# The down projection's fifth block product made as seven of halved blocks, and two products' activations stored split

## The chip, the core and the metric

The program runs on one core of one Trainium2 chip. The metric is device microseconds of one execution. The engines are named as in the profile: PE is TensorE's matmul, PEld its weight load, DVE is VectorE, ACT is ScalarE, POOL is GpSimd, SP issues most of the DMAs. Lnnn is a line of the kernel before, unless a passage says that it shows the kernel after.

## The reference, cut to what matters

SEQ and D_MODEL are 1024, D_FF is 4096, and everything is float32. The block's first sub-layer (a gated mixer of pooling and attention) gives x; the change is all in the second:

```python
h2 = _rmsnorm(x, g_mlp_pre[l])
ff = jnp.einsum('bsf,fd->bsd',
                jnp.square(jax.nn.relu(jnp.einsum('bsd,df->bsf', h2, w_up[l]))), w_down[l])
x = x + _rmsnorm(ff, g_mlp_post[l])
```

Below, x1 is x ahead of this sub-layer, f the squared relu (4096 by 1024, stored by columns of D_FF), and w the down weights.

## The kernel before

**Stages.** The mixer runs to about 470 us of the profiled execution, the up part, which makes f, to about 779, and the down part, which makes ff and the output, to the end.

**Precision.** PE gets operands that are split in two: a rounded high half, which ACT casts (L101), and the rest, which DVE subtracts (L104). A product of two such operands takes three passes: high by high, and the two mixed ones. Every split of 128x1024 thus costs a cast on ACT and a subtraction on DVE.

**Seven block products.** The down matrix product, 2 by 2 blocks, is made as seven block products with sums of blocks for operands (the Winograd form), in place of eight. The seven are numbered 1 to 7 and run in the order of the list `PRODUCTS`, which before is 1, 5, 2, 3, 6, 7, 4. Each goes over the inner dimension in eight steps (NS = 8). A step of a normal product loads one block of f and one of w, 128x1024 each, splits both, and makes 24 matmuls of 128x512 (`down_mm`, L2075) into four PSUM banks. There are 56 steps, numbered j = 0 to 55 through the products.

**One halved product.** The sixth product is again made as seven products of halved blocks (`quarters`, `quarters_mm` L2055, `quarters_close`): 42 matmuls of 128x256 in a step instead of 24 of 128x512, into seven half banks. Its step needs four splits: f1 (the block of f, 1024 elements), f2 (three sums of quarters of f, 768, made in the up part and kept in `spill`), w1 (three quarters of w, 512 and 256), and w2 (four sums of quarters of w, 1024, called T). The T sums are three DVE operations of 512, 256 and 256 (L2009 to L2011), each needing the one before. When its last step is done, `quarters_close` adds the seven results into u with one ACT copy and eight DVE operations (L2062 to L2069).

**Who adds to whom.** The second product is added onto the banks of the first, the third onto those of the fifth. ACT copies the banks out at their ends: u from the first, v from the fifth, c11 from the second, c12 from the third. After the sixth and seventh, DVE sums these (`after_sixth`, `after_seventh`).

**Sums of weight blocks.** The blocks of w stay in SBUF as B11, B12, B21, B22 (eight of each, pool rp of 24 tiles). The fifth needs B12 - B11 (L1978, in its own steps); near the end of the third `differences` makes B22 - B11 and B22 - B12 (L2005, L2007) and the T sums; `last_weights` (L2016) takes one more difference during the seventh and fourth.

**Order and buffers.** Operands of step j+2 are issued in step j (AHEAD = 2). Split operands of f lie in pool wp (six slots "wh"), those of w in pool ga (six), raw blocks from DRAM in four buffers "raw". A load into a buffer, or a split into a slot, waits until its last reader is done. A scheduler orders each engine's instructions, except for stretches under `manual_schedule`, where the named engines run in the written order: DVE from the sixth product on, and PE, ACT and DVE for the sixth's last step and close.

**Up part.** f is made tile by tile in pairs. A function `store` for each pair, run a little later, makes the sums of blocks of f that the down products need and stores them to `f_dram`: seven blocks of 512 columns for each pair, the eighth of them (the sums for f2) to `spill`. While a tile is made, DVE also sums and splits the up weights.

**x1.** In the fifth product's steps `square_x1` loads a tile of x1 into a raw buffer and ACT squares it (L2104), for the last norm.

## Time and profile before

| | |
|---|---|
| median of 3 runs | 1090.79 us (1090.67 to 1090.97) |
| the profiled execution | 1091.0 us, its span 1089.2 |
| mean granted clock of TensorE | 0.999 |
| up part, 470 to 779 us | PE busy 309.00 of 309.00, DVE 219.74, ACT 174.85 |
| down part, 779 to the end | PE busy 302.35 of 310.20, DVE 237.48, ACT 163.05 |

The chain of waits is a list of stretches of work, each released by the one above; a row has its start, its length and what it was. A row of a timeline has the start, the length, the engine, the line, the operation with output and inputs by name, its shape and how many alike followed each other; a bracket tells how long the engine had been idle before it and what ended that. A row of a table of windows has, for each window, its length and then PE, PEld, DVE, ACT and POOL's busy time in it. The costliest groups have busy time, mean ns of one instruction, and the idle time before the group's instructions with what ended it. Of DMA issues, the last number is the median time in us from issue to landing.

### The profile page before, as it was taken

What the parts mean: (1) busy time and instruction counts of PE and PEld (TensorE: products, weight loads), DVE (VectorE), ACT (ScalarE), POOL (GpSimd) and SP (SyncE); (2) the same over time, 40 slices, a digit from 0 to 9 for tenths busy, and PEclk for the clock granted to TensorE, in tenths of its full rate; (3) what the DMA queues carried; (4) which work ended last, traced back from release to release, by engine and by line L of the source; (5) the groups of instructions that cost most, each with busy time, mean ns of one, the idle gap of its engine ahead of it and who ended that gap; (6) DMA issues with size and microseconds to landing.
All of it is one profiled execution on the core that took longest, in us unless ns stands there. A gap on an engine that the chain in (4) does not pass through costs nothing.

```text
span 1089.2 us, 14332 instructions
## 1 busy us (share of the span) xinstructions
PE 1079.7 (99%) x5211; PEld 903.5 (83%) x5211; DVE 849.2 (78%) x1194; ACT 625.5 (57%) x1029; POOL 86.2 (8%) x142
## 2 busy tenths in 40 slices
PE   9999999999999999999999999999999999999997
PEld 8888888888888888888888888888888888898885
DVE  6688888989897887889876766665657867579996
ACT  7567886456654257567665554555446535476543
POOL 0354411100100012100000000000000000000000
PEclk9999999999999999999999999999999999999999
DMA  9666889679965776832566534445597873379622
GB/s 333 201 174 175 214 251 350 184 233 315 268 213 171 223 191 137 288 117 77 185 227 227 205 143 174 160 150 216 177 391 272 299 265 118 101 234 318 218 78 78
DMA packets 100921, 227.36 MB, mean 209 GB/s; under 512 B 10481, under 2 KB 28017, under 8 KB 100849
## 3 DMA queue, kind: packets, MB, share of 16 engines
q1 hardware_dynamic: 84416, 189.46, 50.8%
q0 software_dynamic: 10528, 16.78, 8.8%
q10 hardware_dynamic: 5904, 20.19, 4.8%
q8 instruction: 41, 0.67, 0.3%
q14 instruction: 32, 0.25, 0.1%
HBM read 161.38 MB, written 63.97 MB: 207 GB/s over the span
## 4 chain that ended last, share of the span: by engine, by line
PE 75%; DVE 4%; ACT 1%; issue 1%; DMA 1%; ACTq 0%; DVEq 0%
PE mm L583 18%; PE at L583 15%; PE at L2075 12%; PE mm L2075 11%; PE mm L1523 5%; PE mm L494 3%; PE at L2055 2%; PE at L1523 2%; PE at L1251 2%; PE mm L2055 2%; PE mm L1251 1%; PE mm L496 1%; PE at L1569 1%; DMA st<-in_w_g_dram 1%; DVE xf L2121 0%
## 5 line engine op out<-in xcount | busy, mean ns | idle before, releaser
L2075 PE MATMUL at<-ar,wh 128*128 128x512 f32 x552 | 126.0, 389 | 0.2 <-DVE ar L104 0.2
L2075 PEld LDWEIGHTS at<-ar,wh 128*128 128x128 f32 x552 | 103.4, 188 | 22.1 <-DVE ar L104 0.6
L2075 PE MATMUL mm<-ar,wh 128*128 128x512 f32 x528 | 120.5, 389 | 0.0
L2075 PEld LDWEIGHTS mm<-ar,wh 128*128 128x128 f32 x528 | 99.1, 188 | 20.5
L101 ACT CAST wh<-raw 128x1024 fp32r<-128x1024 f32 (+1 forms) x58 | 59.2, 1023 | 86.2 <-PE at L2075 37.0
L104 DVE TENSOR_TENSOR wh<-st,wh 128x512 fp32r<-128x512 f32 (+1 forms) x103 | 74.4, 733 | 38.9 <-ACT wh L101 34.3
L104 DVE TENSOR_TENSOR wh<-raw,wh 128x1024 fp32r<-128x1024 f32 (+1 forms) x58 | 68.4, 1186 | 40.8 <-ACT wh L101 40.6
L583 PE MATMUL mm<-T,wx 128*128 128x512 f32 x375 | 90.3, 389 | 0.0
L583 PEld LDWEIGHTS mm<-T,wx 128*128 128x128 f32 x375 | 70.4, 188 | 14.6
L583 PE MATMUL mm<-gr,wh 128*128 128x512 f32 x321 | 77.2, 391 | 0.0
L101 ACT CAST wh<-st 128x512 fp32r<-128x512 f32 (+2 forms) x102 | 65.8, 654 | 19.2 <-PE at L583 4.6
L583 PEld LDWEIGHTS mm<-gr,wh 128*128 128x128 f32 x321 | 59.9, 188 | 12.2
L583 PE MATMUL mm<-T,wh 128*128 128x512 f32 x267 | 66.0, 389 | 0.0
L104 DVE TENSOR_TENSOR ar<-B,ar 128x1024 fp32r<-128x1024 f32 (+2 forms) x51 | 50.9, 1011 | 14.7 <-ACT ar L101 14.4
L583 PE MATMUL at<-gr,wh 128*128 128x512 f32 x243 | 59.0, 389 | 0.0
L583 PE MATMUL mm<-x,wh 128*128 128x512 f32 x240 | 58.9, 394 | 0.0
L583 PEld LDWEIGHTS mm<-T,wh 128*128 128x128 f32 x267 | 50.1, 188 | 10.4
L101 ACT CAST ar<-B 128x1024 fp32r<-128x1024 f32 (+2 forms) x51 | 44.1, 882 | 19.3 <-PE mm L2055 6.4
L583 PEld LDWEIGHTS at<-gr,wh 128*128 128x128 f32 x243 | 45.6, 188 | 9.5
L583 PEld LDWEIGHTS mm<-x,wh 128*128 128x128 f32 x240 | 44.2, 188 | 9.6 <-ACT f L692 0.2
L583 PE MATMUL at<-T,wx 128*128 128x512 f32 x213 | 52.0, 389 | 0.0
L583 PEld LDWEIGHTS at<-T,wx 128*128 128x128 f32 x213 | 40.0, 188 | 8.3
(529 smaller groups left out, 2264.5 us busy)
## 6 DMA issues: line engine op xcount, KB each, us to landing
raw<-f_dram SPq DMA_DIRECT2D x52, 512.0 KB, 4.7
B<-in_w_dn_dram SPq DMA_DIRECT2D x32, 512.0 KB, 6.5
f_dram<-g SPq DMA_DIRECT2D x28, 512.0 KB, 2.8
st<-in_w_up_dram SPq DMA_DIRECT2D x24, 512.0 KB, 4.5
g<-spill_dram SPq DMA_DIRECT2D x17, 512.0 KB, 5.7
f_dram<-g ACTq DMA_DIRECT2D x17, 512.0 KB, 2.9
st<-in_w_g_dram SPq DMA_DIRECT2D x16, 512.0 KB, 4.7
g<-in_w_up_dram SPq DMA_DIRECT2D x15, 512.0 KB, 4.8
```

The source lines that it names most:

```text
L101: act.copy(hi, src)
L104: return eng.tensor_tensor(lo, src, f32(hi), ALU.subtract)
L494: pe.matmul(bs[th], whi[:, k, :], rhs(k, hl, th), start=k == 0 and hl == 0, stop=False)
L496: pe.matmul(bs[th], wlo[:, k, :], rhs(k, 0, th), start=False, stop=k == nk - 1)
L583: pe.matmul(b, w[wh][:, kt, :], x_, start=not after and kt == 0 and j == 0, stop=kt == 3 and j == 2, skip_group_check=after)
L1251: pe.matmul(b, w[wh][:, kt, :], xo[xh][:, kt, :], start=not after and kt == 0 and j == 0, stop=kt == 1 and j == 2, skip_group_check=after)
L1523: pe.matmul(bs[t], Am[a][k][ah][:, t * P:(t + 1) * P], Wm[w][k][wh], start=not after and k == 0 and j == 0, stop=k == 3 and j == 2, skip_g ...
L1569: pe.transpose(b[:, i, :], hs[4 * th + i][:, k * P:(k + 1) * P], ident)
L2055: pe.matmul(part[q][:, t, :], o[fs][fh][:, fk, t * P:(t + 1) * P], o[ws][wh][:, wk, :], start=q not in ONTO and (s_, t, j) == (0, 0, 0), s ...
L2075: pe.matmul(bs[t], fo[fh][:, k2, t * P:(t + 1) * P], wo_[wh][:, k2, :], start=not after and s2 == 0 and k2 == 0 and j == 0, stop=(s2, k2) ...
```

## The change

**Order.** The products run as 1, 2, 5, 3, 6, 7, 4, so that the second follows the first, and the fifth, now halved like the sixth, comes behind these two. Steps 0 to 15 are the first and second, 16 to 23 the fifth, 24 to 31 the third, 32 to 39 the sixth, 40 to 47 the seventh, 48 to 55 the fourth. The fifth's close makes v in seven DVE operations; the third has banks of its own and is added to v by DVE at its end (c12).

**Split activations.** `store` splits two more blocks, those of the seventh and the third, and stores both halves: nine blocks for a pair. For these products the halves are loaded straight into slots "wh", and no split of f is made in the down part. It also makes the quarter sums for the fifth's f2.

**Placement.** All of the down part's DVE work but the last step is now in the written order. Loads of weight blocks (`loads`), sums of weight blocks (`sums`) and the rest (`ends`, among it the x1 squares, now in steps 24 to 31) are each given step numbers.

```diff
     def store():
...
-                dve.tensor_tensor(s2[:, 256:], s2[:, :256], s2[:, 256:], ALU.subtract)
-                s2_even.append(s2)
+                for b in (t[:, 0, :], s2):
+                    dve.tensor_tensor(b[:, 256:], b[:, :256], b[:, 256:], ALU.subtract)
+                evens.append(t)
             else:
...
+                for i, a, b in ((5, t0[:, 0, :], t[:, 0, :]), (6, t0[:, 1, :], s2)):
+                    e = g32([3, 256])
+                    dve.tensor_tensor(e[:, 1, :], b[:, 256:], a[:, 256:], ALU.subtract)
+                    dve.tensor_tensor(e[:, 0, :], e[:, 1, :], a[:, :256], ALU.add)
+                    dve.tensor_tensor(e[:, 2, :], b[:, :256], e[:, 1, :], ALU.subtract)
+                    q.dma_start(e_dram(i, m // 4), e)
+            q.dma_start(fd[:, 5:7, :], t)
+            q.dma_start(fd[:, 0, :], f[:, :512])
+            for c, src in ((1, f[:, 512:]), (7, s4)):
+                parts = gr([2, 512])
+                split(parts[:, 0, :], parts[:, 1, :], src)
+                q.dma_start(fd[:, c:c + 2, :], f32(parts))
...
+    WITH_PARTS = (7, 3)
...
     def operands(i, s_):
-        if i == 1 and s_ in early_raw:
+        if i in WITH_PARTS:
+            fo = wslot([2, 512]), wslot([2, 512])
+            for c, t in enumerate(fo):
+                behind[:] = [nc.sync.dma_start(f32(t), f_block(A_OF[i] + c, s_))]
+            ft = None
...
-        split(*fo, ft)
-        behind[:] = [split(*wo_, wt)]
+        if ft is not None:
+            split(*fo, ft)
+        split(*wo_, wt)
...
+    def first_sum(s_):
+        dve.tensor_tensor(res["B11", s_], res["B12", s_], res["B11", s_], ALU.subtract)
+
+    def next_sum(n, s_):
+        dve.tensor_tensor(res[n, s_], res["B22", s_], res[n, s_], ALU.subtract)
...
-            elif i == 5:
-                act.copy(v[t], bs[t])
...
-    PRODUCTS = (1, 5, 2, 3, 6, 7, 4)
+    PRODUCTS = (1, 2, 5, 3, 6, 7, 4)
+    HALVED = (5, 6)
...
+    LOADS = (("B11", 4, 3), ("B12", 5, 8), ("B22", 15, 8), ("B21", 41, 8))
...
+    def sums(j):
...
+        if at(8):
+            first_sum(j - 8)
+        if at(9):
+            quarter_sums(j - 9)
+        if at(18):
+            next_sum("B12", j - 18)
+        if at(22):
+            next_sum("B11", j - 22)
+        if at(24):
+            quarter_sums(j - 24)
+        if at(42):
+            last_sum(j - 42)
...
+    def ends(j):
...
+        if 24 <= j < 24 + NS:
+            square_x1(j - 24)
...
+    def down_step(j, i, s_):
...
+        if i in HALVED and last:
+            with tc.manual_schedule(engines=CORE):
+                quarters_mm(i, s_)
+                quarters_close(i)
+            ahead(j)
+            sums(j)
...
+        else:
+            sums(j)
+            ahead(j)
+        loads(j)
...
-    fd = nc.dram_tensor("f_dram", (NF // 2, P, 7, 512), F32, kind="Internal").ap()
+    fd = nc.dram_tensor("f_dram", (NF // 2, P, 9, 512), F32, kind="Internal").ap()
```

Three places in the order of instructions. The first is DVE behind the fifth's close in the kernel after, steps 23 and 24, where L104 is the subtraction of a split, L2009 a sum of weight blocks (`next_sum`), and L2017 to L2019 the T sums:

```order
L104 TENSOR_TENSOR ar_8395<-B_1247_7896,ar_8394 128x1024
L2009 TENSOR_TENSOR B_1189_7609<-B_1298_8170,B_1189_7609 128x1024
L2009 TENSOR_TENSOR B_1150_7400<-B_1247_7896,B_1150_7400 128x1024
L2009 TENSOR_TENSOR B_1197_7652<-B_1309_8237,B_1197_7652 128x1024
L2009 TENSOR_TENSOR B_1158_7440<-B_1265_7969,B_1158_7440 128x1024
L2017 TENSOR_TENSOR T_8402<-B_1143_7362 128x512
L2018 TENSOR_TENSOR T_8402<-B_1143_7362,T_8402 128x256
L2019 TENSOR_TENSOR T_8402<-B_1143_7362,T_8402 128x256
L104 TENSOR_TENSOR ar_8411<-B_1265_7969,ar_8410 128x1024
```

Before, the same sums (L2005, L2007) stand in the second and third products, where the scheduler put them among the splits of f and w (here those of the second):

```order
L2007 TENSOR_TENSOR B_1154_7473<-B_1255_8087,B_1154_7473 128x1024
L2005 TENSOR_TENSOR B_1105_7199<-B_1261_8123,B_1105_7199 128x1024
L104 TENSOR_TENSOR wh_7750<-raw_7745,wh_7749 128x1024
L104 TENSOR_TENSOR ar_7752<-raw_7747,ar_7751 128x1024
L2007 TENSOR_TENSOR B_1161_7513<-B_1261_8123,B_1161_7513 128x1024
```

So the sums moved to the end of the halved fifth and the start of the third, and four of them and a T now stand between the weight splits of steps 25 and 26.

The second place is ACT at the end of the fifth in the kernel after. L2116 is a square of x1, L2069 the copy that opens the close:

```order
L101 CAST wh_8219<-raw_8217 128x768
L2116 ACTIVATE raw_8442,nsq<-raw_8442 128x1024
L101 CAST wh_8229<-raw_8215 128x1024
L101 CAST ar_8227<-B_1145_7390 128x512
L101 CAST ar_8227<-B_1145_7390 128x256
L101 CAST ar_8287<-B_1235_7840 128x1024
L2116 ACTIVATE raw_8485,nsq<-raw_8485 128x1024
L2116 ACTIVATE raw_8527,nsq<-raw_8527 128x1024
L2069 COPY st_8379<-mm_7900 128x512
```

The first square moved from the normal fifth to a place between the cast of f2 and those of f1 and w1 of step 23, and two more stand ahead of the copy.

The third place is DVE behind the first `store` of the up part, with the splits of the up weights (wx, wh). Before:

```order
L1631 TENSOR_TENSOR g_5075<-f_first,g_5074 128x512
L104 TENSOR_TENSOR wx_5118<-ws_5112,wx_5118 128x512
L1635 TENSOR_TENSOR g_5074<-g_5074 128x256
L613 TENSOR_TENSOR g_5097<-g_5097,at_5084 128x512
L104 TENSOR_TENSOR wx_5122<-st_5055,wx_5122 128x512
```

And after:

```order
L1631 TENSOR_TENSOR g_5075<-f_first,g_5074 128x512
L1636 TENSOR_TENSOR g_5074<-g_5074 128x256 x2
L104 TENSOR_TENSOR gr_5084<-g_4608,gr_5084 128x512
L104 TENSOR_TENSOR wx_5126<-ws_5120,wx_5126 128x512
L104 TENSOR_TENSOR wx_5130<-st_5055,wx_5130 128x512
L104 TENSOR_TENSOR gr_5088<-g_5075,gr_5088 128x512
```

The two splits of `store` (gr) stand among those of the next weights, one of them ahead of wx.

## The prediction

> **What bounds the kernel now.** I read first the page's busy times, then the chain of waits, then the timelines of TensorE and VectorE where the products of the last stage meet.

> ```profile
> span 1089.2 us, 14332 instructions
> PE 1079.7 (99%) x5211; PEld 903.5 (83%) x5211; DVE 849.2 (78%) x1194; ACT 625.5 (57%) x1029; POOL 86.2 (8%) x142
> ```

> TensorE is busy for 99% of the span, so time can only go where matmuls go, and any wait that the change lets TensorE see is added whole. VectorE has 22% free on average; that says nothing about one stage. The chain of waits (start, length, what) shows what a product of the last stage costs:

> ```profile
> 822.82 43.52 PE mm L2075 x192
> 866.34 43.52 PE at L2075 x192
> 909.86 43.52 PE mm L2075 x192
> 953.38 2.87 PE at L2055 x24
> ...
> 993.85 4.30 PE at L2075 x19
> 998.15 1.14 DVE wh L104
> 999.28 1.15 DVE ar L104
> 1000.47 37.47 PE at L2075 x164
> ```

> A normal product is 192 matmuls in 43.52 us, 226.7 ns each and 5.44 us a step. The sixth, the halved one, begins at 953.38 and its successor's first matmul is in the timeline of TensorE:

> ```profile
> 993.69 6.58 PE L2075 MATMUL at<-ar,wh 128*128 128x512 f32 x28
> 1000.47 2.79 PE L2075 MATMUL at<-ar,wh 128*128 128x512 f32 x11 [0.21 <-DVE ar L104]
> ...
> 1037.78 4.47 PE L2075 MATMUL mm<-ar,wh 128*128 128x512 f32 x19
> ```

> The sixth takes 993.69 - 953.38 = 40.31 us: 336 matmuls of 128x256 at 120 ns, 5.04 us a step. The seventh, from 993.69 to 1037.78, takes 44.09 us where 43.52 would do; 0.57 us is lost in its second step, which waited for VectorE. What VectorE did there:

> ```profile
> 993.15 0.68 DVE L2062 TENSOR_TENSOR st<-st,at 128x512 f32<-128x512 f32 x1
> ...
> 997.46 0.68 DVE L2069 TENSOR_TENSOR u<-u,st 128x512 f32<-128x512 f32 x1
> 998.06 1.22 DVE L104 TENSOR_TENSOR wh<-raw,wh 128x1024 fp32r<-128x1024 f32 x1
> 999.20 1.22 DVE L104 TENSOR_TENSOR ar<-B,ar 128x1024 fp32r<-128x1024 f32 x1
> 1000.34 1.22 DVE L104 TENSOR_TENSOR wh<-raw,wh 128x1024 fp32r<-128x1024 f32 x1
> ```

> The eight operations of the close take 4.91 us, and the splits of the next step's two operands stand behind them. Operations in a row follow each other in 1.14 us though each lasts 1.22: 0.08 us of each lies beside its neighbour. So a 128x1024 operation costs 1.14 in a row, and by the same overlap a 128x512 one 0.61, a 128x256 one 0.34.

> **How full VectorE is in a halved product**, by its timeline in one step of the sixth:

> ```profile
> 968.51 1.03 DVE L104 TENSOR_TENSOR ar<-B,ar 128x512 fp32r<-128x512 f32 x2
> 969.45 2.10 DVE L104 TENSOR_TENSOR wh<-raw,wh 128x1024 fp32r<-128x1024 f32 x2
> 971.47 1.22 DVE L104 TENSOR_TENSOR ar<-T,ar 128x1024 fp32r<-128x1024 f32 x1
> 973.54 1.03 DVE L104 TENSOR_TENSOR ar<-B,ar 128x512 fp32r<-128x512 f32 x2 [0.86 <-ACT ar L101]
> ```

> A step's splits take w1 0.95, f1 1.14, f2 0.87 and w2 1.14: 4.10 of 5.04 us, and 0.86 is idle, in which it waits for TensorE to free a buffer. VectorE is about half a step ahead, no more, since the operand buffers hold no more.

> **The change, part by part.** The sum starts from the profiled execution's own 1091.0 us (1.8 outside its span); the median of the runs is 1090.79, so the two agree within 0.02%.

> (1) The fifth product has 336 matmuls of 128x256 in place of 192 of 128x512: 43.52 - 40.32 = **-3.20 us**. A matmul of half the columns costs 120 ns and not 113.3, so 2 x 120 - 226.7 = 13.3 ns of each is fixed by these rows. [...]

> (2) The seventh's activations come split from DRAM, so of the three splits behind the sixth's close only that of the weights is left. The wait of **-0.57** goes. What is late next there is the load itself: the two halves of a step go straight into operand buffers that are free only when the step two before has run, so the first block of the seventh has 5.04 us.

> ```profile
> raw<-f_dram SPq DMA_DIRECT2D x52, 512.0 KB, 4.7
> raw<-x_dram SPq DMA_DIRECT2D x8, 512.0 KB, 5.1
> ```

> Two such loads, issued behind each other on SP, land 4.7 us after issue or a little later: 0 to 0.8 us of wait, no less than nothing as no buffer is free sooner. I take **+0.4**, between the ends. VectorE's and ACT's saved splits in the third and seventh are off the path, beyond the stretch in (4).

> (3) The fifth now follows the second, whose end ACT copies out (four copies and four squares) ahead of the fifth's casts. The timeline of ACT shows that pattern after the second in before:

> ```profile
> 909.11 1.06 ACT L2248 COPY c<-at 128x512 f32<-128x512 f32 x2
> ...
> 911.68 0.21 ACT L2081 ACTIVATION_READ_ACCUMULATOR junk<-c 128x1 f32 x1
> 911.77 1.05 ACT L101 CAST wh<-raw 128x1024 fp32r<-128x1024 f32 x1
> ```

> There a cast stood until 911.77, some 2 us into the next product, with nobody waiting. A halved step needs its f1 2.4 us after its start. So the first step can wait 0 (if casts slip in between) to 0.95 us (two more squares ahead); I take **+0.35**.

> (4) The stretch from the fifth into the third is the term that decides. The sums of weight blocks (one 128x1024 operation each, 1.14) are now placed by step number: one in each of steps 18 to 21, two in each of 22 to 25, and from step 24 on also the sums for the sixth's T:

> ```profile
> 907.72 0.69 DVE L2009 TENSOR_TENSOR T<-B 128x512 f32<-128x512 f32 x1
> 908.44 0.42 DVE L2010 TENSOR_TENSOR T<-B,T 128x256 f32<-128x256 f32 x1
> 908.90 0.42 DVE L2011 TENSOR_TENSOR T<-B,T 128x256 f32<-128x256 f32 x1
> 909.25 0.69 DVE L2084 TENSOR_TENSOR c<-c,bc 128x512 f32<-128x512 f32 x1
> ```

> Each of these waits for the one before, so the three take 1.53. VectorE's order is fixed as written, so I add it from the start of step 19 to the split that step 26 needs: w1 and f1 of 19, 2.1; four times a sum and a step's splits, 4 x (1.14 + 4.10) = 21.0; two sums, 2.3; the weights of step 24, 1.1; the fifth's close, seven operations, 4.3; the weights of 25, 1.1; four sums, 4.6; T, 1.5; the weights of 26, 1.2. That is 39.2 us. TensorE uses up in the same stretch five halved steps, two normal ones and the four matmuls that stand ahead of the first one needing that split: 5 x 5.04 + 2 x 5.44 + 0.9 = 37.0. So TensorE waits **+2.2 us**, spread over steps 21 to 26. The low end is 0, if some of those sums find idle time that I have not seen; the high end counts all 43 operations at full length instead of overlapped, 43 x 0.08 = 3.4 more, 5.6 in all. I take 2.2, because the rows at 998.06 to 1000.34 show the overlap in just such a run of operations.

> (5) The squares of x1 move from the fifth's steps, where they were in a normal product, to steps 24 to 31, and are recorded so that the first stands on ACT ahead of the casts of step 23's f1 and w1, and two more ahead of the copy that opens the close. Their loads go through the same four raw buffers.

> ```profile
> L2104 ACT ACTIVATE raw<-raw 128x1024 f32<-128x1024 f32 x8 | 8.5, 1060 | 4.8 <-DMA raw<-x_dram 4.8
> ```

> ACT already sat 4.8 us for these loads in before, with a normal product around it as cover. Behind the waiting square are now the casts for step 23, for which TensorE waits 2.4 us into it; on SP the first blocks of the third wait behind the x1 loads. The load is issued once f2 of step 22 is split, 5.1 us before it lands. What of this goes beyond the 2.2 of (4) is bounded by 0 (ACT waits while VectorE is late anyway) and 1.7 (step 23 alone waits 2.25, 0.55 of which is in (4)); **+0.5**, nearer to the lower end because both waits fall in the same steps.

> (6) The up part splits two blocks more in every pair of tiles and makes one or three more 128x256 sums: 2 x 0.61 + 2 x 0.34 = 1.9 us of VectorE a pair, 2.2 where nothing overlaps, and two casts on ACT. The two pairs at 500 to 537 have almost nothing free (the columns behind the bounds are PE, weight load, VectorE, ACT):

> ```profile
> 500.00:518.00 18.00, 18.00 (x85) 15.00 (x84) 18.00 (x25) 12.09 (x18) 0.00 (x0) 1.00 0.30 91
> 518.00:537.00 19.00, 19.00 (x85) 15.74 (x84) 17.80 (x31) 13.48 (x22) 0.00 (x0) 1.00 0.46 167
> 537.00:556.00 19.00, 19.00 (x85) 15.73 (x85) 10.96 (x20) 10.75 (x17) 0.00 (x0) 1.00 0.67 233
> ```

> 1.2 us are free in those 37 and 3.8 to 4.4 are added; 8.0 are free in the 19 behind. If the late work is the stores', it drains there and costs nothing; if weight splits wait behind it, up to 3.2. I take **+0.5**.

> Sum: 1091.0 - 3.20 - 0.57 + 0.4 + 0.35 + 2.2 + 0.5 + 0.5 = 1091.2 us. Most of what TensorE no longer does, it waits.

> **The rivals.**
> - VectorE keeps up. The waits of (4), (5) and (6) are hidden: 1091.2 - 2.2 - 0.5 - 0.5 = 1088.0. For it: the 849.2 us of VectorE leave room on both sides of the stretch. Against it: its order is fixed, and nothing lets it start a step's splits earlier than the buffers come free.
> - The x1 squares hold ACT, ending slower: the first square waits for its load while step 23's casts stand behind it, and the copy of the close behind two more. It decides from the point where the load lands later than 2.4 us into step 23 less two casts. Then (5) costs 2.5 and not 0.5: 1093.2. For it: the 4.8 us row above. Against it: three of the raw loads ahead could be early.
> - The up part's backlog reaches TensorE: 2.6 instead of 0.5, 1093.3. For it: the windows at 500 to 537. Against it: those windows hold work that can be put off, and TensorE had no gap there.
> - Every small operation pays its full length in the stretch: (4) costs 5.6, 1094.6. [...] The rows of the close at 993.15 to 998.06 speak against it, since they overlap.

> That the fifth isn't halved at all is excluded by the order of TensorE's instructions, which has 336 of 128x256 for it.

> **How the numbers follow.** A measurement of this kernel can tell about 0.2%, 2.2 us, from no change. The forecast, 1091.2, has 0.38 and lies within it (1088.6 to 1093.0). VectorE keeping up, 1088.0, has 0.29 and is faster by more. The x1 squares have 0.17, the up part 0.11, full-length operations 0.05; these three are slower by more, 0.33 together. The range reaches from a little under the first rival, 1087.4, to a little over the fourth's 1094.6, 1095.4: it leaves out at its low end the case that nothing waits at all, 1087.2, and at its high end two rivals at once.

> **What would show it.** In the profile of the changed kernel the fifth should take 40.3 us plus its own waits. (4) is right if TensorE's idle time in the second half of the fifth and the first three steps of the third is near 2 us and is ended by VectorE's splits of weights; if ACT's cast or an x1 load ends it, (5) was the greater. (2) is right if the seventh's first step waits for a load for less than a microsecond and its second step not at all. (6) shows as idle TensorE between 500 and 560, released by VectorE. The forecast is wrong if VectorE has idle time within the stretch, or if TensorE's gaps stand somewhere else altogether, such as in the second product, where sums for the fifth are now made.

## The result, and the profile after

The changed kernel takes **1109.44 us** (median of 4 runs, 1107.02 to 1112.63) against 1090.79 before: a ratio of 1.0173, 95% interval 1.0147 to 1.0199. It is 1.7% slower, and outside the predicted range.

The page of the changed kernel, its first lines and the row of TensorE's clock:

```profile
span 1107.8 us, 14938 instructions
PE 1086.9 (98%) x5355; PEld 911.4 (82%) x5355; DVE 893.0 (81%) x1301; ACT 637.9 (58%) x1062; POOL 84.4 (8%) x142
...
PEclk9999999999999999999989999999999999999998
```

VectorE has 44 us more to do and ACT 12. TensorE's busy time went up by 7.2 us although its matmuls need 3.2 us less: some of them ran slower. There is an 8 in the row of the clock, in the 21st slice, near 560 us, where before there was a 9. Where the 18.6 us of span are, from the starts of stages in TensorE's timelines:

```profile
789.65 2.88 PE L583 MATMUL at<-ar,wh 128*128 128x512 f32 x12
792.38 4.42 PE L2087 MATMUL at<-gr,wh 128*128 128x512 f32 x18
...
883.28 3.04 PE L2061 MATMUL mm<-ar,wh 128*128 128x256 f32 x24
...
1011.64 0.70 PE L2087 MATMUL mm<-ar,wh 128*128 128x512 f32 x2
```

L583 is the up part, L2087 a normal down product, L2061 a halved one.

| stretch | before | after | difference |
|---|---|---|---|
| to the end of the up part (779.14; after: 792.38, less six down matmuls that stand among those of the up part, 1.36 us) | 779.1 | 791.0 | +11.9 |
| first and second normal product | 87.0 | 92.3 | +5.2 |
| the next three products (before: two normal and the sixth, 866.2 to 993.7; after: the fifth, third and sixth) | 127.5 | 128.4 | +0.9 |
| the last two and the end | 95.5 | 96.2 | +0.7 |

Before, the second place in the row "first and second" was the fifth's; both are normal products. The place that the prediction was about, the third row, came out 1 us above its forecast there. Nearly all of the loss stands ahead of it. TensorE's gaps there, from its timeline:

```profile
565.08 0.73 PE L583 MATMUL mm<-T,wx 128*128 128x512 f32 x2 [3.10 <-ACT wx L101]
568.32 4.21 PE L583 MATMUL mm<-T,wh 128*128 128x512 f32 x9 [1.82 <-ACT g L612]
...
597.51 0.73 PE L583 MATMUL mm<-T,wx 128*128 128x512 f32 x2 [0.44 <-ACT wx L101]
599.80 3.91 PE L583 MATMUL mm<-T,wh 128*128 128x512 f32 x9 [1.03 <-ACT g L612]
...
809.99 0.73 PE L2087 MATMUL at<-ar,wh 128*128 128x512 f32 x2 [2.32 <-ACT ar L101]
811.25 4.14 PE L2087 MATMUL at<-ar,wh 128*128 128x512 f32 x10 [0.53 <-DVE ar L104]
```

Four gaps in the up part make 6.4 us, two in the first product 2.85. Behind the gaps matmuls are slow: nine in 4.21 us, where nine take 2.0. The table of windows of TensorE alone (length, busy time, granted clock, DMA share, GB/s) shows why:

```profile
564.00:566.00 2.00, 0.92 (x4) 1.00 0.35 131
566.00:568.00 2.00, 0.50 (x2) 0.50 0.00 0
568.00:570.00 2.00, 1.68 (x4) 0.50 0.71 276
570.00:572.00 2.00, 2.00 (x6) 0.50 1.01 391
572.00:574.00 2.00, 2.00 (x9) 0.80 0.97 315
```

The gap begins at 561.98 (565.08 - 3.10); from 566 on the clock stands at half, and it is back at full near 572.8 (0.80 is the mean of that row): some 7 us. So the gaps cost 6.4 us in the up part and what follows them 5.5 more; in the first product 2.85 and 2.4. What follows is half clock (10.2 us of it in the up part, 3.4 in the first product, half of which is lost) and a slower start behind each gap (two matmuls in 0.73 us at 565.08 and 597.51, where two at 561.36, ahead of the first gap, took 0.61).

**The first gap.** It ends with ACT's cast of a sum of up weights (L532, L535), and that sum needs a weight load. SP's queue in the changed kernel:

```profile
555.10 0.92 SPq L1651 DMA_DIRECT2D f_dram<-gr  x2
556.13 1.26 SPq L523 DMA_DIRECT2D g<-in_w_up_dram  x1
```

and in the kernel before:

```profile
551.40 0.48 SPq L523 DMA_DIRECT2D g<-in_w_up_dram  x1
551.99 0.58 SPq L523 DMA_DIRECT2D st<-in_w_up_dram  x1
553.99 0.33 SPq L523 DMA_DIRECT2D g<-in_w_up_dram  x1
```

The load (L523) into a buffer g is issued 4.7 us later, behind the two stores of split halves (L1651), and the next one, at 553.99 before, only at 569.56. The pool of these buffers has 17, and each pair of tiles now takes two more of them, until the stores have landed; but no weight load between 480 and 780 us is seen to wait for the landing of such a store.

The late load alone doesn't explain the gap. VectorE's timeline at the sum, in the changed kernel:

```profile
561.56 0.69 DVE L625 TENSOR_TENSOR g<-g,at 128x512 f32<-128x512 f32 x1 [5.15 <-PE at L583]
562.62 0.69 DVE L532 TENSOR_TENSOR ws<-g 128x512 f32<-128x512 f32 x1 [0.37 <-DMA g<-in_w_up_dram]
```

The sum waited 0.37 us for its load, and ACT, busy without a break from 562.28 on, came to the cast 0.38 us after the sum was made. Before, the same chain, from L625 at 556.30 to the cast at 559.03, is as long (2.7 against 2.85 us), but TensorE has 12 matmuls (at<-T,wx, from 556.10) to make meanwhile. In the changed kernel these 12 ran at 550.53 already, ahead of those on wh, whose operand ACT's copy L612 made at 555.11: it stands behind the two casts of stored halves, which waited 2.41 us for VectorE's sums. Before it was made at 549.00. The gaps of 1.82 and 1.03 us end with this copy too, again behind these casts.

**Why the gap in the first product.** What SP waited for between 780 and 812 us in the changed kernel, the longest row (total, times, longest), and the first weight load of the down part in its timeline:

```profile
SPq L1962 <- DVE g L1644: 12.3, 1, 12.3
```

```profile
802.86 0.38 SPq L1962 DMA_DIRECT2D B<-in_w_dn_dram  x1
```

The load's tile lies over the buffer of the last store's quarter sums (L1644); when they were made, it waited 2.7 us more, until they had landed in `spill`. It went out at 802.86, 11.9 us after the up part's end; before, at 784.77, 5.6 us after, for there another buffer lay under it.

### The profile page after: what moved, and what is told of

Same layout as the page of the kernel before. It is cut to its first block, busy times and chain, and to the rows that moved or that the text cites. A ratio compares the mean times of both kernels' runs of the same rounds, so it can differ in the third digit from the quotient of the medians.

```text
span 1107.8 us, 14938 instructions
## 1 busy us (share of the span) xinstructions
PE 1086.9 (98%) x5355; PEld 911.4 (82%) x5355; DVE 893.0 (81%) x1301; ACT 637.9 (58%) x1062; POOL 84.4 (8%) x142
## 4 chain that ended last, share of the span: by engine, by line
PE 88%; DVE 5%; DMA 4%; ACT 2%; issue 1%; SPq 0%; DVEq 0%; ACTq 0%
PE mm L583 25%; PE at L583 17%; PE at L2087 12%; PE mm L2087 6%; PE mm L1523 5%; PE at L2061 3%; PE mm L494 3%; PE mm L2061 3%; PE sc L182 2%; PE at L1523 2%; PE at L1251 2%; PE mm L191 2%; PE mm L182 2%; PE mm L1251 1%; PE mm L496 1%; DMA wh<-f_dram 1%
## 5 line engine op out<-in xcount | busy, mean ns | idle before, releaser
L2087 PE MATMUL at<-ar,wh 128*128 128x512 f32 x588 | 144.2, 393 | 4.2 <-ACT ar L101 2.3
L2087 PEld LDWEIGHTS at<-ar,wh 128*128 128x128 f32 x588 | 111.2, 190 | 29.0 <-ACT ar L101 4.3
L104 DVE TENSOR_TENSOR wh<-st,wh 128x512 fp32r<-128x512 f32 (+1 forms) x103 | 74.9, 736 | 38.8 <-ACT wh L101 34.7
L583 PE MATMUL mm<-T,wx 128*128 128x512 f32 x375 | 92.0, 390 | 3.5 <-ACT wx L101 3.5
L583 PEld LDWEIGHTS mm<-T,wx 128*128 128x128 f32 x375 | 70.7, 189 | 19.1 <-ACT wx L101 4.4
L101 ACT CAST wh<-raw 128x1024 fp32r<-128x1024 f32 (+1 forms) x50 | 48.9, 981 | 55.5 <-PE at L2087 40.8
L583 PE MATMUL mm<-gr,wh 128*128 128x512 f32 x321 | 77.2, 391 | 0.0
L101 ACT CAST wh<-st 128x512 fp32r<-128x512 f32 (+2 forms) x102 | 65.9, 653 | 19.3 <-DVE st L539 6.0
L2087 PE MATMUL mm<-ar,wh 128*128 128x512 f32 x300 | 76.9, 390 | 0.1
L583 PE MATMUL mm<-T,wh 128*128 128x512 f32 x267 | 70.4, 407 | 2.9 <-ACT g L612 2.9
L104 DVE TENSOR_TENSOR wh<-raw,wh 128x1024 fp32r<-128x1024 f32 (+1 forms) x50 | 56.4, 1136 | 17.5 <-ACT wh L101 17.3
L583 PEld LDWEIGHTS mm<-gr,wh 128*128 128x128 f32 x321 | 59.9, 188 | 12.2
L101 ACT CAST ar<-B 128x1024 fp32r<-128x1024 f32 (+2 forms) x59 | 42.8, 757 | 43.2 <-DMA B<-in_w_dn_dram 10.7
L2087 PEld LDWEIGHTS mm<-ar,wh 128*128 128x128 f32 x300 | 56.2, 188 | 12.3 <-DMA wh<-f_dram 0.5
L104 DVE TENSOR_TENSOR ar<-B,ar 128x1024 fp32r<-128x1024 f32 (+2 forms) x59 | 49.3, 859 | 20.5 <-ACT ar L101 20.4
L583 PEld LDWEIGHTS mm<-T,wh 128*128 128x128 f32 x267 | 51.9, 196 | 15.7 <-ACT g L612 4.8
L583 PE MATMUL at<-gr,wh 128*128 128x512 f32 x243 | 59.0, 389 | 0.0
L583 PE MATMUL mm<-x,wh 128*128 128x512 f32 x240 | 58.9, 394 | 0.0
L583 PEld LDWEIGHTS at<-gr,wh 128*128 128x128 f32 x243 | 45.6, 188 | 9.5
L583 PE MATMUL at<-T,wx 128*128 128x512 f32 x213 | 53.1, 390 | 0.0
L583 PEld LDWEIGHTS mm<-x,wh 128*128 128x128 f32 x240 | 44.2, 188 | 9.6 <-ACT f L692 0.2
L2061 PE MATMUL mm<-ar,wh 128*128 128x256 f32 x336 | 47.5, 285 | 0.7 <-DVE ar L104 0.4
## 6 DMA issues: line engine op xcount, KB each, us to landing
raw<-f_dram SPq DMA_DIRECT2D x36, 512.0 KB, 4.3
B<-in_w_dn_dram SPq DMA_DIRECT2D x32, 512.0 KB, 6.4
wh<-f_dram SPq DMA_DIRECT2D x32, 512.0 KB, 5.2
f_dram<-gr SPq DMA_DIRECT2D x30, 512.0 KB, 4.2
st<-in_w_up_dram SPq DMA_DIRECT2D x24, 512.0 KB, 4.3
g<-spill_dram SPq DMA_DIRECT2D x17, 512.0 KB, 5.7
st<-in_w_g_dram SPq DMA_DIRECT2D x16, 512.0 KB, 5.3
f_dram<-g ACTq DMA_DIRECT2D x16, 512.0 KB, 2.7
```

Source lines behind the costliest of these rows:

```text
L101: act.copy(hi, src)
L104: return eng.tensor_tensor(lo, src, f32(hi), ALU.subtract)
L583: pe.matmul(b, w[wh][:, kt, :], x_, start=not after and kt == 0 and j == 0, stop=kt == 3 and j == 2, skip_group_check=after)
L2061: pe.matmul(part[q][:, t, :], o[fs][fh][:, fk, t * P:(t + 1) * P], o[ws][wh][:, wk, :], start=q not in onto and (s_, t, j) == (0, 0, 0), s ...
L2087: pe.matmul(bs[t], fo[fh][:, k2, t * P:(t + 1) * P], wo_[wh][:, k2, :], start=not after and s2 == 0 and k2 == 0 and j == 0, stop=(s2, k2) ...
```

## The experiments

Each time stands against the kernel before, run on the same chip (1090.4 to 1090.9 in each set). Where a kernel has the down part of the change, "the stretch" is from the fifth's first matmul to the sixth's end: 128.4 us in the change, 124.2 by its matmuls (2 x 40.32 + 43.52). Kernels with the same down part differed there by up to 2 us (128.4 to 130.3), so less is not read.

**1. The stored splits, away.** Blocks stored whole, and split in the down part again:

```diff
-            q.dma_start(fd[:, 0, :], f[:, :512])
-            for c, src in ((1, f[:, 512:]), (7, s4)):
-                parts = gr([2, 512])
-                split(parts[:, 0, :], parts[:, 1, :], src)
-                q.dma_start(fd[:, c:c + 2, :], f32(parts))
+            q.dma_start(fd[:, 0:2, :], f.rearrange("p (a b) -> p a b", b=512))
+            q.dma_start(fd[:, 7, :], s4)
...
-    WITH_PARTS = (7, 3)
+    WITH_PARTS = ()
```

> The change, but the blocks of f for the third and seventh are stored whole as before and split in the down part again; all else as changed (fifth halved, order, sums, x1). Theory A (the loss is made in the up part by the stored splits, directly and by the half clock behind the gaps): TensorE has no gap between 540 and 640 us, the up part ends at 779 to 781 us as in the kernel before, and the time falls by 10 or more, to about 1095 (3.2 gained by the halving, about 7 lost in the stretch from the fifth to the third, where three more splits of 1.14 come in). Theory B (the loss comes from halving the fifth and the written order of the down part): the time stays above 1104.

Measured: 1095.94 (ratio 1.0045, 1.0028 to 1.0062). No gap in the up part, which ends where it ended before. The fifth starts at 866.26, as the third product in order does before. All 17 us ahead of the fifth are the stored splits'. The waits of TensorE from 480 us on are in the down part:

```profile
PE at L2084 <- DVE ar L104: 4.1, 3, 2.6
PE mm L2058 <- DVE ar L104: 0.4, 1, 0.4
```

So Theory A holds. It leaves 5 us: without split blocks VectorE is late in the third, and the stretch is 132.6.

**2. The stores on GpSimd's queue.**

```diff
-                q.dma_start(fd[:, c:c + 2, :], f32(parts))
+                nc.gpsimd.dma_start(fd[:, c:c + 2, :], f32(parts))
```

> The change, with the two stores of split halves of each pair issued by GpSimd's queue and not by SP's or ACT's. If SP's order is what delays the up weights (their load stands behind two stores that wait for the splits): the gaps at 562 to 568 and 597 to 600 us go or halve, the up part ends at 780 to 785 us, time about 1098 to 1102. If it is the buffers (a weight load waits for a buffer that a store frees on landing, and stores on GpSimd's queue land no earlier): gaps as before or longer, time 1107 or more.

Measured: 1103.21 (1.0111, 1.0095 to 1.0126), 6 us less than the change. The up part's gaps shrank to 3.7 us in all (1.9, 1.0, 0.8) and its last matmuls start 5.5 us sooner (784.16 for 789.65). Here the sum L532 waited 6.67 us for its weight load, and the gap of 1.9 followed. With the stores off SP's queue about half of the up part's loss goes (5 of 11.9 us), a third of the whole; the first product's gap of 2.3 us stays.

**3. Other memory under the first load.**

```diff
+    pool.memset(held("pad")[:, 0, :], 0.0)
+    pool.memset(raw_tile()[:, 0, :], 0.0)
     with tc.manual_schedule(engines={mybir.EngineType.DVE}):
```

> The change, with one unused weight tile and one unused raw tile allocated (and cleared by GpSimd) ahead of the down part, so that the first weight load of the first product gets memory that is long free and not that of the last store's sums. If SP stood still until 802.86 us for that memory: the first such load is issued by 800 at the latest, the gap of 2.3 + 0.5 us at 808 to 811 goes with the half clock behind it, and the time falls by about 5, to 1104. If the load was late for another reason (the queue's other waits, the DMA engines): unchanged within 1.

Measured: 1104.48 (1.0134, 1.0114 to 1.0153), 5.0 less. In its trace the first load is issued at 796.04, and of the gap 0.19 us is left:

```profile
813.08 2.14 PE L2087 MATMUL at<-ar,wh 128*128 128x512 f32 x8 [0.19 <-DVE ar L104]
```

The fifth starts at 878.31, 5.0 us sooner, 0.45 of it from the up part. So the memory under the first tiles was the cause of 4.5 of the 5.2 us in the second row of the table. The execution that was profiled is the slowest of the four, 1108.81: behind the fifth's start it lost again what it had gained, 130.3 us in the stretch and 1.54 at the seventh's start.

**4 and 5. What a gap costs.** First, idle operations put into VectorE's order in the kernel before:

```diff
             with given(i):
+                for _ in range({1: 10, 5: 14}.get(s_, 0)):
+                    dve.tensor_tensor(c11[3], c11[3], c11[3], ALU.max)
```

> The kernel before, with 10 and 14 idle operations of VectorE (128x512, 0.61 us each in a row) put ahead of the splits in the second and sixth steps of the seventh product; results unchanged. If a gap costs only itself, the time rises by the idle time of TensorE that the trace shows, and the granted clock stays 1.00. If a gap of some 2 us or more is followed by a stretch at half clock, as at 566 to 573 us in the changed kernel, the windows behind it show a clock near 0.5 for 3 to 6 us and the time rises by the idle time plus half of that, about 2 us more for each gap.

Measured: 1091.53, and no gap: the scheduler moved these operations, which hang on nothing, ahead into idle time. It decides nothing. Then on the loaded block itself:

```diff
+        for _ in range({(7, 3): 6, (4, 1): 10}.get((i, s_), 0)):
+            dve.tensor_tensor(ft, ft, ft, ALU.max)
         split(*fo, ft)
```

> The kernel before, with 6 idle operations of VectorE (1.14 us each) on the block of f of the seventh's fourth step and 10 on that of the fourth's second step, results unchanged. If a gap costs only itself, the granted clock stays at 1.00 behind the gaps and the time rises by TensorE's idle time. If a gap of over 2 us is followed by half clock, the windows behind show 0.5 for 3 to 6 us, and the time rises by the idle time and about 2 us more for each such gap.

Measured: 1109.28, +18.9. TensorE's timeline at its gaps, and the table of windows behind the first one:

```profile
1014.61 2.07 PE L2077 MATMUL at<-ar,wh 128*128 128x512 f32 x4 [4.08 <-ACT wh L101]
1017.01 28.42 PE L2077 MATMUL at<-ar,wh 128*128 128x512 f32 x116 [0.32 <-DVE ar L104]
1053.36 1.20 PE L2077 MATMUL mm<-ar,wh 128*128 128x512 f32 x4 [2.49 <-ACT wh L101]
1055.75 29.50 PE L2077 MATMUL mm<-ar,wh 128*128 128x512 f32 x116 [1.20 <-DVE ar L104]
```

```profile
1014.00:1016.00 2.00, 1.39 (x3) 0.54 0.00 0
1016.00:1018.00 2.00, 1.68 (x4) 0.50 0.49 94
1018.00:1020.00 2.00, 2.00 (x6) 0.50 1.03 371
1020.00:1022.00 2.00, 2.00 (x8) 0.76 0.95 316
```

The four gaps are 8.1 us of the 18.9. Behind each of the two pairs TensorE stood at half clock for 6.8 us, which costs 3.4 each time, more than the 2 us that were expected; some 3 us more stand behind the last matmul, where VectorE's own work came late. So in a kernel that has none of the change, a wait alone brings the half clock. It begins some 3.5 us after the first gap's start (1014.61 - 4.08 = 1010.53, and 0.54 from 1014 on). The second pair brought it too, though its gaps are of 2.49 and 1.20 us, with 1.2 us of matmuls between them: no single wait as long as the first's 4.08 was needed.

**6. One buffer for both high halves**, the low halves written over their blocks:

```diff
...
+            high = gr([2, 512])
+            for c, src in ((0, f[:, 512:]), (1, s4)):
+                split(high[:, c, :], src, src)
+            q.dma_start(fd[:, 0:2, :], f.rearrange("p (a b) -> p a b", b=512))
+            q.dma_start(fd[:, 8, :], s4)
+            q.dma_start(fd[:, 6:8, :], f32(high))
```

> The change, with each pair's stored splits written otherwise: the low halves over the blocks they come from, both high halves in one buffer, so that a pair takes one buffer of the pool more than before the change and not two, and four stores of halves and blocks instead of four plus one; the same splits on ACT and VectorE. If buffers and the number of stores ahead of the weight loads make the up part's gaps: the gaps shrink to under 2 us in all, the up part ends at 779 to 783 us, time 1098 to 1101. If the additional work of VectorE and ACT makes them: the gaps stay near 6 us and the time at 1107 or more.

Measured: 1109.83 (1.0174, 1.0157 to 1.0191), no gain in all. The up part's gaps fell to 4.2 us (3.2 and 1.0), and its last matmuls start 5.2 us sooner; but the first load of the down part still went out at 802.76, since its tile lay over a buffer of stored halves until these had landed, and that gap grew to 5.8:

```profile
SPq L1963 <- DMA f_dram<-gr: 11.1, 1, 11.1
```

One loss was exchanged for another.

**7 to 9. The stretch from the fifth to the sixth.** Sums of weights later; x1 loads behind those of f; both:

```diff
-        if at(18):
-            next_sum("B12", j - 18)
+        if at(22):
+            next_sum("B12", j - 22)
```

```diff
-        nc.sync.dma_start(t, x1_dram[n])
+        with tc.issue_after(behind[0].ins):
+            nc.sync.dma_start(t, x1_dram[n])
```

> The change, with the sums B22 - B12 placed in steps 22 to 29 and not 18 to 25: four sums fewer (4.6 us of VectorE) ahead of the weights' split of step 26. The stretch from the first matmul of the fifth to the end of the sixth took 128.3 us in the changed kernel where its matmuls need 124.2. If VectorE's sums set that loss: 124.5 to 126, and VectorE has idle time in the fifth. If the x1 loads and squares set it: 128 or more, with the wait for the blocks of f at the start of the third as before.

> The change, with each x1 load issued behind the loads of f for the third, so that no square stands on ACT ahead of step 23's casts. If the x1 loads and squares set the loss of 4.1 us in the stretch from the fifth to the sixth's end: the wait of 1.34 us for the first blocks of the third goes, ACT's idle 0.71 us of VectorE too, and the stretch takes 125 to 126.5 us. If VectorE's sums set it: 127.5 or more, with waits that VectorE's splits end.

> The change, with the later sums and the later x1 loads together. Theory: each of the two hides the other, since either alone left the stretch from the fifth to the sixth's end at 127.5 to 129.4 us (128.3 in the changed kernel). Then both together take it to 125 to 126, near the 124.2 of its matmuls. If something else sets it (the loads of split blocks, TensorE's own order): 127.5 or more again.

Measured, times 1110.62, 1110.52 and 1105.17 (one run each, beside a change that varies from 1107.0 to 1112.6); the stretch 128.4, 127.5 and 127.0. Fewer sums alone bring nothing. The later x1 loads bring 1 us, and both 1.4, under what was expected (125 to 126). With x1 later, the wait of 1.34 us for the first blocks of the third went and a wait for VectorE's split of 1.1 us came in the third:

```profile
938.95 0.74 PE L2087 MATMUL at<-ar,wh 128*128 128x512 f32 x2 [1.10 <-DVE ar L104]
```

So each hid a part of the other; some 3 us stay above the matmuls' time with both.

**10 and 11. Can the kernel with whole blocks win?** T sums from step 26, or the sums B22 - B12 on GpSimd:

```diff
-        if at(24):
-            quarter_sums(j - 24)
+        if at(26):
+            quarter_sums(j - 26)
```

```diff
-        dve.tensor_tensor(res[n, s_], res["B22", s_], res[n, s_], ALU.subtract)
+        eng = pool if n == "B12" else dve
+        eng.tensor_tensor(res[n, s_], res["B22", s_], res[n, s_], ALU.subtract)
```

> The kernel with whole blocks stored (unsplit), the later x1 loads, and the sums for the sixth's T placed in steps 26 to 33 and not 24 to 31. The loss of unsplit against its matmuls stood in the third, where VectorE's splits ended waits of 4.1 us and half clock followed. If VectorE's order there was the cause: the waits at 909 to 925 us fall to under 1 us and the time to 1088 to 1091. If VectorE simply has too much work in that stretch, wherever it stands: 1093 or more.

> The kernel with whole blocks stored, the later x1 loads, and the eight sums B22 - B12 made by GpSimd and not VectorE (9 us of VectorE less in the fifth and third). If VectorE's amount of work sets the loss and GpSimd does a sum in 5 us or less: the waits in the third fall to 1 to 2 us and the time to 1088 to 1091. If GpSimd is slower, or slows VectorE beside it: 1093 or more.

Measured: 1095.37 (1.0042, 1.0027 to 1.0057) and 1102.67 (1.0107, 1.0090 to 1.0124). With later T sums the waits in the third fell to 2.5 us and the sixth got 1.6 us of new ones: VectorE has too much to do there, wherever it stands. GpSimd made a sum in 2.6 to 2.7 us, fast enough, and yet this was 7 us slower than whole blocks without it (experiment 1, which differs in the x1 loads too). VectorE's and GpSimd's timelines beside each other:

```profile
889.61 2.08 DVE L104 TENSOR_TENSOR wh<-raw,wh 128x1024 fp32r<-128x1024 f32 x2
891.61 3.39 DVE L104 TENSOR_TENSOR ar<-T,ar 128x1024 fp32r<-128x1024 f32 x1
```

```profile
891.32 2.61 POOL L2007 TENSOR_TENSOR B<-B,B 128x1024 f32<-128x1024 f32 x1 [1.92 <-DVE wh L104]
```

VectorE's subtraction, 1.22 us at 884.83 and at 898.03, took 3.39 when it was started while GpSimd's sum ran, and ended behind it. Both operations read two tensors of SBUF.

**12. All remedies at once**: 3, 6, 9 and the later T sums, in one kernel.

> The change with all of its losses taken on at once: one buffer for the high halves, unused tiles ahead of the first weight loads, later sums, later x1 loads, T sums from step 26. If the losses found are all there are and they add up: the up part ends at about 787 (gaps of 4 us and half clock stay), no gap in the first product, 125 to 126 us from the fifth to the sixth's end; time 1094 to 1098. If taking one away shows another behind it: 1102 or more.

Measured: 1101.70 (1.0104, 1.0089 to 1.0119), 7.7 less than the change and above the expected 1094 to 1098. The fifth starts at 874.43, 8.9 us sooner than in the change; the stretch is 127.4; but from the sixth's end on it takes 98.8 us where the change takes 96.2, with a new wait of 1.8 us for VectorE in the fourth. The losses add up only in part.

**13 to 15. What a stored split does to the up part.** To the kernel with whole blocks, one thing each was added: the splits' work, into a free half of a buffer; as many and as large stores; or the two buffers, with splits and stores of 16 columns.

```diff
...
+            for src in (f[:, 512:], s4):
+                act.copy(spare.bitcast(F32R), src)
+                dve.tensor_tensor(spare.bitcast(F32R), src, spare, ALU.subtract)
...
```

```diff
             q.dma_start(fd[:, 0, :], f[:, :512])
...
+            q.dma_start(fd[:, 1:3, :], f.rearrange("p (a b) -> p a b", b=512))
+            q.dma_start(fd[:, 7, :], s4)
+            q.dma_start(fd[:, 8, :], s4)
...
```

```diff
+            for src in (f[:, 512:], s4):
+                parts = gr([2, 512])
+                split(parts[:, 0, :16], parts[:, 1, :16], src[:, :16])
+                q.dma_start(fd[:, 8, :32].rearrange("p (a b) -> p a b", b=16), f32(parts[:, :, :16]))
...
```

> The kernel with whole blocks stored (unsplit, 1095.9 us, no gap in the up part), with the two splits of each pair made on ACT and VectorE all the same, into a free half of a buffer, and not stored or used. If the up part lost its 11.9 us by the work of ACT and VectorE: gaps near 560 and 600 us, time 1102 or more. If by buffers and queue alone: no gap over 0.5 us in the up part, time 1095 to 1098 (the later end of the last store may delay the first product by 1 or 2).

> The same kernel with as many and as large stores for each pair as in the change (a second store of a block's two halves and of the sums, 0.5 MB more a pair... of what lies there), no splits and no more buffers. If the stores' number and bytes on SP's queue make the loss: gaps near 560 and 600 us, time 1102 or more. If not: no gap over 0.5 us, 1095 to 1098.

> The same kernel with two more buffers taken for each pair, as in the change, each with a split and a store of 2 x 16 columns only: the buffers are held until that store lands, and the stores stand in SP's queue behind the splits, but neither work nor bytes are added to speak of. If the weight loads wait for buffers and behind those stores: gaps of 3 us or more near 560 us, time 1102 or more, even though nothing else is added. If not: 1095 to 1098, and the loss needs all three together.

Measured: 1098.08, 1097.62 and 1104.61 (1.0065, 1.0062 and 1.0130; the last one's interval 1.0113 to 1.0147). The fifth starts at 867.5, 867.6 and 873.7, against 866.3 with whole blocks and 883.3 in the change. Work alone costs 1.2 us, of which 0.1 in the up part; stores alone cost 1.3, all in the up part; buffers with almost nothing in them cost 7.4, 5.4 of it there. TensorE's waits from 480 to 860 us in the last kernel:

```profile
PE mm L583 <- ACT g L612: 1.6, 1, 1.6
PE at L583 <- ACT wx L101: 1.0, 1, 1.0
...
PE mm L583 <- ACT f L603: 0.7, 1, 0.7
...
PE mm L583 <- ACT wx L101: 0.5, 1, 0.5
```

The gaps stand at 563 to 595 us, as in the change, but half clock followed none of them (clock 1.00 in every 10 us from 540 to 1090). One at a time the three make 10 of the 17 us; the other 7 come when they are together, and the half clock of the change (5.5 and 2.4 with the slow starts) is of that size.

The 7.4 can't all be put down to buffers. Both small stores of a pair go to the same columns of `f_dram`, so that the second stands on SP until the first has landed, which the change hasn't. What SP waited for from 480 to 780 us in this kernel:

```profile
SPq L1650 <- DMA f_dram<-gr: 14.5, 14, 2.3
```

And the longest gap, 1.58 us, ends with ACT's copy L612, which stands behind the two casts of 16 columns as it does behind the full ones in the change; with work alone the scheduler put this copy ahead of the second cast, where it ran at 550.90, as early as with whole blocks (551.01). Each of these kernels was ordered anew, and none holds the order still. So how the up part's loss divides among buffers, the stores' place on SP and the casts' place on ACT stays open.

None of these kernels is faster than the kernel before; the best, with whole blocks and later T sums, is 0.4% slower.

## Why the prediction was wrong

It said 1091.2 us, range 1087.4 to 1095.4. By its own steps:

(1) The halved fifth: right. Its matmuls take the 120 ns that the sixth's took, 3.2 us less than a normal product.

(2) The seventh: right. The wait in its second step is gone, and its first step now waits for its load: five matmuls of the change from 1011.64 on take 1.59 us where 1.13 would do, 0.45 lost, with +0.4 said. In the later kernels with stored splits that wait is 0.6 to 0.8 us in four and 1.0 and 1.5 in two, over the 0.8 said as the most; in one ACT's cast is waited for, 1.3.

(3) No wait at the fifth's start: 0 instead of +0.35.

(4) and (5) were too small: 2.7 us said; the stretch took 4.2 longer than its matmuls (128.4 against 124.2). Three gaps make 2.07 of that:

```profile
919.95 1.58 PE L2061 MATMUL mm<-ar,wh 128*128 128x256 f32 x11 [0.40 <-DVE ar L104]
922.82 1.45 PE L2061 MATMUL mm<-ar,wh 128*128 128x256 f32 x10 [0.33 <-DVE wh L104]
927.04 0.47 PE L2087 MATMUL at<-ar,wh 128*128 128x512 f32 x1 [1.34 <-DMA wh<-f_dram]
```

The rest are the slow starts behind them and some ten waits too short to show as gaps, some 0.35 us of them in the sixth. VectorE's splits account for about 2, as (4) said. The longest gap was ended by the first blocks of the third, behind the x1 loads on SP: that is (5)'s mechanism, at 1.3 to 1.6 us and not 0.5. VectorE's own time was nearly as worked out; from its timeline, the end of it:

```profile
937.73 1.22 DVE L104 TENSOR_TENSOR ar<-B,ar 128x1024 fp32r<-128x1024 f32 x1
```

The split for step 26 ended at 938.95 (937.73 + 1.22). Step 19 began three halved steps after 883.28, at 898.4: 40.6 us, where the sum said 39.2; 0.7 of the difference is VectorE's wait for ACT behind an x1 square. Operations in a row overlapped, as taken (1.13 to 1.14 us from start to start at 899.90 to 902.17, each 1.22 long).

(6) **is the step that failed**: the up part, "+0.5", "up to 3.2", came out as 11.9. Its bound counted VectorE's free time alone, from the windows at 500 to 537. But the work by itself cost the up part 0.1 us in the order that it had in experiment 13. What the step left out is where the stored splits stand in orders that are fixed: their stores ahead of the next weight load on SP (4.7 us later), their casts ahead of ACT's copy L612, which TensorE's next matmuls need (6.1 us later). That the stored splits make the loss is shown by experiment 1; how it divides among these places and the buffers that the splits hold is open. The rival on the up part had the right place and the wrong mechanism, and so the wrong price, 2.6.

Two terms were missing. No step looked at the **start of the down part**: the last store runs longer, and the memory of the first weight load lay under it, +5.2 us, of which the two unused tiles took 4.5 away. And every wait was priced as **its own length**: here the gaps of 9.3 us ahead of the fifth were followed by some 8 us more of half clock and slow starts. The prediction said that any wait is "added whole"; it is added with what follows it.

The last row of the table, +0.7 although the seventh's wait of 0.57 went: 0.1 of it is in the matmuls, where 0.45 came for the load and 0.15 more for a split in the fourth. The other 0.55 stands behind the last 512-column matmul, from 1098.02 to the end, and wasn't settled.

## What to carry to other kernels

Work that is moved out of a full stage into one that "has room" is paid for there in more than engine time: list what stands behind its stores in the queue that also loads, what stands behind its operations on each engine of fixed order, and the buffers that it holds and until when. Where a change alters which buffers a stage uses last, look at which memory the next stage loads into first. Where TensorE is busy all the time, price a wait of 2 us or more, or two shorter ones close together (0.44 and 1.03 us in the change), as the wait plus the 1.7 or 3.4 us that half clock can cost behind it (half of the 3.41 or 6.83 us that it lasted in the change).

## What the runs showed of the hardware

```profile
922.55:925.97 3.42, 1.40 (x6) 1.00 0.53 131
925.97:929.38 3.41, 3.41 (x10) 0.50 0.44 177
```

```profile
921.45:924.86 3.41, 1.81 (x8) 1.00 0.15 24
924.86:928.27 3.41, 2.41 (x11) 1.00 0.81 296
```

```profile
596.72:600.13 3.41, 1.94 (x7) 1.00 0.62 201
600.13:603.54 3.41, 3.41 (x9) 0.50 1.02 399
```

  The gap of 2.59 us leaves 2.02 us idle in one step, the one of 2.60 is cut by the grid into 1.60 and 1.00. In all traces, from 470 to 1085 us, 17 steps at full clock have 1.95 us or more of idle time, and half clock follows all of them (in the change 2.50 and 2.18 us, ahead of 565.99 and 811.75). Between 1.47 and 1.85 us it follows three (1.47 in the change, 1.52 and 1.61, each of two gaps) and not the others, and below that none (1.34 in the change, from 924.39 on). So in these traces 1.95 us of idle time in one step was always enough and 1.47 to 1.85 sometimes, and what looks like chance is mostly the gap's place on the grid. It fits that the changed kernel's runs spread over 5.6 us and those of the kernel before over 1.2 us.
- **GpSimd's sums held VectorE** in the kernel of experiment 11. Beside the one of 2.61 us at 891.32 a subtraction of VectorE took 3.39 us for 1.22 and ended 1.07 us behind it; beside the one of 2.71 us at 886.70 two subtractions of 128x512 took 3.23 us for 1.03. All of these operations read two tensors.
